# Shift and scale of six channel tiles by VectorE's product and sum, low parts of these rows on GpSimd, h by ScalarE

## The chip, the cores and the metric

The kernel runs on one core of one Trainium2 chip. The metric is the device time of one execution in microseconds (us). A core has five engines that run their own instruction rows and wait for each other by semaphores: TensorE (PE; its weight loads are shown as PEld), VectorE (DVE), ScalarE (ACT), GpSimd (POOL) and SyncE (SP), which here only issues transfers.

## What is computed

One layer of a trunk with two parallel head groups, a bidirectional state-space scan (SSD) and a gated MLP, over 256 latent tokens and 256 context tokens of 2048 channels. What matters here is its beginning: the modulation of the normalised rows and the first columns of the input projection.

```
shift, scale, gate       = split(silu(c)     @ w_ada + b_ada, 3)      # c: (2048,), w_ada: (2048, 3 * 2048)
shift_c, scale_c, gate_c = split(silu(c_ctx) @ w_ada + b_ada, 3)
hc = rmsnorm(ctx, g_pre) * (1 + scale_c) + shift_c
zc = hc @ w_in[:, :XBC_W + DT_W]
hx = rmsnorm(x, g_pre) * (1 + scale) + shift
zx = hx @ w_in
... scan, gating, output projection ...
return x + gate * rmsnorm(mixed, g_post)
```

All inputs are float32.

## The kernel before

The 2048 channels are 16 tiles of 128 (kt = 0 to 15), with channels on partitions; the 512 tokens (context, then latent) are columns. Every matrix product of the projections is made of three products of rounded halves: hi is the value rounded by ScalarE (`copy` to fp32r), lo the rest (`tensor_tensor`, subtract), and `mm3` (L136) adds hi x hi, hi x lo and lo x hi.

The front of the program, up to `st.close()`, goes like this. x is loaded in four pieces, squared (on VectorE and ScalarE by turns, L264 and L266) and summed over channels by products with ones (L268); `rb` (L282) is the root-mean-square factor of each token, the same in all partitions, kept in a segment of `y`, a tile that is not in use yet. Between the groups of products stand products of ones as warm-up (`warm`).

Then the streamed projections run over kt. `row_steps` (L325) writes out the order for TensorE, VectorE, ScalarE and GpSimd by hand, one list of steps per channel tile:

- `("a", ci)` is `ada_mm` (L204): one chunk of w_ada, 1 MiB, against silu(c) and silu(c_ctx) on TensorE. A unit of `UNITS` is one or two channel tiles; it sums shift and scale of its tiles over all 2048 rows of w_ada in one PSUM bank, four groups of partitions side by side. Two chunks belong to a tile.
- `("f", u)` is `ada_fin` (L218): VectorE transposes the bank in blocks of 32 (L222) into `adat`, ScalarE makes from it ha = g_pre * (1 + scale) (L224) and hb = shift (L226), each 128 x 2 for the two token halves.
- `("h", kt)` is `make_h` (L304): for each half VectorE makes x * ha * rb (L307), ScalarE adds hb and rounds (hhi, L310), VectorE makes the rest hlo (L312).
- `("s", kt)` is `split_st` (L294): ScalarE rounds the row of w_in for dt and seven column tiles (`wst`, 128 x 960, L299), VectorE makes its low parts (L300, L301).
- `("m", i)` are the products, psdt (L362, L363) first and then seven psx tiles.

A list ends each step with the rest of its "m". In the last one, `dt_tok` copies psdt out and multiplies it by `fold` (pstok, L320), a sum of two halves of the identity that is made at L165.

SyncE's row of loads is in program order: `ada_load` and `wst_load` stand ahead of each kt, three chunks and two w rows ahead; six buffers hold w_ada chunks, three hold w rows. Then the program goes on with the other columns of w_in as a stream of 1 MiB tiles w (hi_w, lo_w), the scan, the gating and the output projection. There, for `gate`, VectorE already makes the third part of c @ w_ada by itself (`gate_tile`, L884): w_ada's columns lie on partitions, the row of silu(c) is broadcast to all partitions, and one `scalar_tensor_tensor` with `accum_out` multiplies and sums along 2048 values.

Of the kernel before, what the change touches and what calls it, by code (L numbers as in the profile page):

```python
# [29 lines left out]
WSSD = (0, 1, 2, 3, 4, 12, 5, 6, 13, 7, 8, 14, 9, 10, 15, 11)  # L30
C_BADA, C_GPRE, C_GSSD, C_GMLP, C_BS, C_CW, C_CB, NPC = 0, 48, 64, 80, 96, 112, 272, 304
# [10 lines left out]
def tile_hybrid_ssd_mlp(  # L42
# [88 lines left out]
    cpool.tile([P, 64], F32, name="cpad")  # L131
# [32 lines left out]
    A = yseg(7)[:, 320:384]  # L164
    nc.vector.tensor_reduce(fold, ident.rearrange("p (g m) -> p m g", g=2), axis=mybir.AxisListType.X, op=ALU.add)  # L165
# [12 lines left out]
    sc2 = stp.tile([P, KT, 2], F32, name="sc2")  # L178
    nc.sync.dma_start(sc2, ccols)
# [5 lines left out]
    ada_raw = {}  # L185


    UNITS = [(0,), (1,)] + [(m, m + 1) for m in range(2, KT, 2)]

    def ada_place(ci):  # L190

        if ci < 4:
            return ci // 2, 64, 8 * (ci % 2), 8
        return ci // 4 + 1, 128, 4 * (ci % 4), 4

    def ada_load(*cs):
        for ci in cs:
            ada_raw[ci] = load_raw(wada[ci], f"ada_{ci}")
# [6 lines left out]
    def ada_mm(ci):  # L205
        u, n, k0, nk = ada_place(ci)
        if k0 == 0:
            ada_ps[u] = spt([P, 512], f"psada{u}")
        ps = ada_ps[u]
        raw = ada_raw.pop(ci)  # L210
        for kk in range(nk):
            k = k0 + kk
            for g in range(4):
                o = (kk * 4 + g) * n
                nc.tensor.matmul(ps[32 * g : 32 * g + 32, 0:n], lhsT=sc[:, k, :], rhs=raw[:, o : o + n],  # L215
                                 start=k == 0, stop=k == KT - 1)

    def ada_fin(u):  # L218
# [4 lines left out]
        for q, kt in enumerate(UNITS[u]):  # L223
            nc.scalar.activation(ha[:, kt, :], tr[:, 64 * q : 64 * q + 2], AF.Identity, bias=bsc1[:, kt : kt + 1],  # L224
                                 scale=pc[:, C_GPRE + kt : C_GPRE + kt + 1])
            nc.scalar.activation(hb[:, kt, :], tr[:, 64 * q + 32 : 64 * q + 34], AF.Identity,  # L226
                                 bias=pc[:, C_BADA + kt : C_BADA + kt + 1])
# [5 lines left out]
    wraw = {}  # L233

    def wst_load(kt):
        w = st3.tile([P, WST], F32, tag="wst", name=f"wst{kt}")
        nc.sync.dma_start(w, wst[kt])
        wraw[kt] = w

    for t in range(4):  # L240
        nc.sync.dma_start(xT[:, 4 * t : 4 * t + 4, :].rearrange("p k t -> p (k t)"), xch[t])
    ada_load(0)
    wst_load(0)
    ada_load(1, 2, 3)
    wst_load(1)
    ada_load(4, 5)

# [9 lines left out]

    warm(2)

    pss = spt([P, TOK], "pss")  # L260
    for k in range(KT):
        sq = yseg((1, 2, 3, 6, 0)[k % 5])
# [6 lines left out]
        if g == 3:  # L269
            warm(1)  # L270


    rb, ss4 = yseg(4), yseg(5)
# [9 lines left out]
    ada_mm(0)  # L283
    ada_mm(1)
# [10 lines left out]
    def split_st(kt):  # L295
# [4 lines left out]
        nc.vector.tensor_tensor(hi[:, 0:64], raw[:, 0:64], hi[:, 64:P].bitcast(F32), op=ALU.subtract)  # L300
        nc.vector.tensor_tensor(lo, raw[:, 64:], hi[:, P:].bitcast(F32), op=ALU.subtract)  # L301
        return hi, lo

    def make_h(kt):  # L304
        sl = (slice(256, 512), slice(0, 256))
        for v, s in enumerate(sl):
            nc.vector.scalar_tensor_tensor(xT[:, kt, s], xT[:, kt, s], ha[:, kt, v : v + 1], rb[:, s],  # L307
                                           op0=ALU.mult, op1=ALU.mult)
        for v, s in enumerate(sl):
            nc.scalar.activation(hhi[kt][:, s], xT[:, kt, s], AF.Identity, bias=hb[:, kt, v : v + 1])  # L310
        for v, s in enumerate(sl):
            nc.vector.scalar_tensor_tensor(hlo[kt][:, s], xT[:, kt, s], hb[:, kt, v : v + 1],  # L312
                                           hhi[kt][:, s].bitcast(F32), op0=ALU.add, op1=ALU.subtract)


    def dt_tok():
        nc.scalar.copy(zdt, psdt)
# [7 lines left out]
    def row_steps(kt):  # L325
# [3 lines left out]
        nxt = [("h", kt + 1), ("s", kt + 1)]  # L329
        if kt == 0:  # L330
            return m[:1] + [("a", 2)] + m[1:2] + [("a", 3)] + m[2:3] + [("f", 1)] + nxt + m[3:] + [("a", 4), ("a", 5)]
        if kt < 3:
            f = [("f", 2)] if kt == 1 else []
            return m[:3] + [("a", 2 * kt + 4)] + m[3:5] + [("a", 2 * kt + 5)] + f + nxt + m[5:]
# [6 lines left out]
        a = [("a", 2 * kt + 4), ("a", 2 * kt + 5)] if kt + 2 < KT else []  # L341
        f = [("f", (kt + 1) // 2 + 1)] if kt % 2 else []
        if kt < 5:
            return m[:2] + a + f + nxt + m[2:]
        return nxt[1:] + a + f + nxt[:1] + m

    def step(kt, what, i):
        if what == "a":
            ada_mm(i)
# [4 lines left out]
        elif what == "s":  # L354
            sp0[i] = split_st(i)
# [13 lines left out]
    sp0[0] = split_st(0)  # L369
    ada_fin(0)  # L370
    make_h(0)
    for kt in range(KT):
        if kt + 3 < KT:
            ada_load(2 * kt + 6, 2 * kt + 7)
        if kt + 2 < KT:
            wst_load(kt + 2)
# [4 lines left out]
        for what, i in row_steps(kt):  # L381
            step(kt, what, i)
# [772 lines left out]
def _layout(i):  # L1155
# [13 lines left out]
    for kt in range(2):  # L1169
        wada[2 * kt : 2 * kt + 2] = ss[:, :, :, kt].reshape(2, 8, P, 256).transpose(0, 2, 1, 3).reshape(2, P, D)  # L1170
# [50 lines left out]
```

## Time and profile before

| | us |
|---|---|
| median of 3 runs (1000.07 to 1000.66) | 1000.56 |
| the profiled execution | 999.99 |
| its span, first to last instruction | 998.3 |
| TensorE busy, share of the span | 977.1 (98%) |
| VectorE busy | 629.9 (63%) |
| ScalarE busy | 493.0 (49%) |
| GpSimd busy | 113.7 (11%) |
| streamed projections' end, first product of the w stream | 134.00 |

The profile is of one execution. Its views: a page of the whole span; the timeline (start in us, length in us, engine, line, operation, out<-in, shape, count, and in brackets the idle time before it and what ended it); stretches of the span with the busy time of each engine; and one line's instructions with their shortest, median and longest duration in ns. A VectorE instruction with `accum_out` shows as two, the second of which reads the accumulator (DVE_READ_ACCUMULATOR). Names are the program's tiles without their numbers.

### The profile page before, as it was taken

To read this page: it belongs to the slowest core of one execution; us is meant where nothing else is said; L and a number is where in the kernel's file an instruction comes from. 1 tells how busy PE (TensorE), PEld (TensorE's weight loads), DVE (VectorE), ACT (ScalarE), POOL (GpSimd) and SP (SyncE) were. 2 spreads that over 40 slices of the span, in tenths; PEclk is the share of its full clock that TensorE was granted. 3 is DMA by queue.
4 is the path that set the end of the run, shared out by engine and by line. 5 is a ranking of instruction groups with operands and counts; after the bars stand their busy time and mean duration, and the time that the engine had idled before them with its cause. 6 is when DMAs were issued, how large, how long until landed. Compare 5 with 4: busy or idle time off the path is not lost.

```text
span 998.3 us, 14183 instructions
## 1 busy us (share of the span) xinstructions
PE 977.1 (98%) x5636; PEld 791.3 (79%) x5636; DVE 629.9 (63%) x944; ACT 493.0 (49%) x759; POOL 113.7 (11%) x162
## 2 busy tenths in 40 slices
PE   7999999999999999999999999999999999999996
PEld 3788888778687878787888888877888888888885
DVE  4344478877977665666667766666565564445636
ACT  4233347666656545544445343455565564346522
POOL 0000003423443222224000000000000000000000
PEclk9999999999999999999999999999999999999998
DMA  9999744333224323235878778674555545556722
GB/s 380 419 417 419 293 175 143 111 127 127 85 85 165 103 112 133 79 127 195 311 283 297 275 258 319 252 274 172 185 173 191 188 169 209 175 207 231 274 85 84
DMA packets 31554, 207.28 MB, mean 208 GB/s; under 512 B 4080, under 2 KB 4208, under 8 KB 7808
## 3 DMA queue, kind: packets, MB, share of 16 engines
q1 hardware_dynamic: 28656, 192.52, 51.5%
q0 software_dynamic: 2112, 12.65, 3.6%
q10 hardware_dynamic: 720, 1.20, 0.3%
q8 instruction: 44, 0.72, 0.3%
q14 instruction: 22, 0.18, 0.1%
HBM read 204.20 MB, written 2.16 MB: 207 GB/s over the span
## 4 chain that ended last, share of the span: by engine, by line
PE 69%; issue 11%; DMA 9%; DVE 8%; POOL 1%; ACT 1%; SPq 0%; DVEq 0%; POOLq 0%; ACTq 0%
PE psx L138 9%; PE psx L140 9%; PE psx L139 9%; PE pa L1026 5%; PE pa L1028 5%; PE pa L1027 5%; DMA gate<-in_wada_dram 5%; PE pm L1073 3%; PE pm L1075 3%; PE pm L1074 3%; PE psada L215 3%; DVE xbc L495 2%; PE pq L1075 2%; PE pq L1073 2%; PE pq L1074 2%
## 5 line engine op out<-in xcount | busy, mean ns | idle before, releaser
L82 DVE TENSOR_TENSOR lo_w<-w,hi_w 128x1024 fp32r<-128x1024 f32 x173 | 210.5, 1224 | 144.3 <-ACT hi_w L81 144.3
L81 ACT CAST hi_w<-w 128x1024 fp32r<-128x1024 f32 x173 | 182.1, 1053 | 202.5 <-PE pa L1028 130.5
L1026 PE MATMUL pa<-hi_w,hhi 128*128 128x512 f32 x512 | 202.5, 395 | 0.0
L1028 PE MATMUL pa<-hi_w,hlo 128*128 128x512 f32 x512 | 199.5, 390 | 0.0
L1027 PE MATMUL pa<-lo_w,hhi 128*128 128x512 f32 x512 | 199.4, 389 | 0.0
L138 PE MATMUL psx<-hhi,hi_w 128*128 128x512 f32 (+1 forms) x400 | 153.5, 384 | 1.3 <-DVE xbc L495 1.3
L140 PE MATMUL psx<-hhi,lo_w 128*128 128x512 f32 (+1 forms) x400 | 146.0, 365 | 0.0
L139 PE MATMUL psx<-hlo,hi_w 128*128 128x512 f32 (+1 forms) x400 | 145.7, 364 | 0.0
L1026 PEld LDWEIGHTS pa<-hi_w,hhi 128*128 128x128 f32 x512 | 96.2, 188 | 20.7 <-issue 1.6
L1028 PEld LDWEIGHTS pa<-hi_w,hlo 128*128 128x128 f32 x512 | 96.1, 188 | 20.2
L1027 PEld LDWEIGHTS pa<-lo_w,hhi 128*128 128x128 f32 x512 | 96.2, 188 | 19.4 <-issue 0.2
L495 DVE SCALAR_TENSOR_TENSOR xbc<-psx,pc,xbc 128x248 f32<-128x248 f32 (+1 forms) x204 | 83.6, 473 | 36.6 <-ACT xbc L479 35.6
L420 DVE TENSOR_TENSOR lo_w<-w,hi_w 128x1024 fp32r<-128x1024 f32 x61 | 78.1, 1287 | 25.0 <-ACT hi_w L414 25.0
L138 PEld LDWEIGHTS psx<-hhi,hi_w 128*128 128x128 f32 x400 | 75.5, 189 | 15.0 <-issue 3.1
L140 PEld LDWEIGHTS psx<-hhi,lo_w 128*128 128x128 f32 x400 | 75.4, 189 | 12.6
L139 PEld LDWEIGHTS psx<-hlo,hi_w 128*128 128x128 f32 x400 | 75.6, 189 | 12.1 <-issue 1.7
L414 ACT CAST hi_w<-w 128x1024 fp32r<-128x1024 f32 x61 | 63.4, 1044 | 26.4 <-PE pa L1028 13.3
L884 DVE SCALAR_TENSOR_TENSOR junk<-gate,cb 128x2048 bf16<-128x2048 f32 x16 | 36.6, 2290 | 24.6 <-DMA gate<-in_wada_dram 24.6
L1073 PE MATMUL pm<-hi_w,hhi 128*128 128x512 f32 x128 | 50.0, 390 | 0.0
L1074 PE MATMUL pm<-lo_w,hhi 128*128 128x512 f32 x128 | 49.9, 390 | 0.0
L1075 PE MATMUL pm<-hi_w,hlo 128*128 128x512 f32 x128 | 49.7, 389 | 0.0
L138 PE MATMUL psx<-hhi,hi_st 128*128 128x512 f32 (+1 forms) x112 | 41.3, 369 | 0.0
(219 smaller groups left out, 1333.7 us busy)
## 6 DMA issues: line engine op xcount, KB each, us to landing
w<-in_wlat_dram SPq DMA_DIRECT2D x64, 1024.0 KB, 4.8
ada<-in_wada_dram SPq DMA_DIRECT2D x32, 1024.0 KB, 14.6
w<-in_wout_dram SPq DMA_DIRECT2D x32, 1024.0 KB, 4.8
w<-in_wxbc_dram SPq DMA_DIRECT2D x25, 1024.0 KB, 4.8
gate<-in_wada_dram SPq DMA_DIRECT2D x16, 1024.0 KB, 5.7
R<-acs POOLq DMA_DIRECT2D x8, 1024.0 KB, 4.9
wst<-in_wst_dram SPq DMA_DIRECT2D x16, 480.0 KB, 14.8
xT<-in_xch_dram SPq DMA_DIRECT2D x4, 1024.0 KB, 8.0
```

Source lines behind the costliest of these rows:

```text
L81: nc.scalar.copy(hi, raw)
L82: nc.vector.tensor_tensor(lo, raw, hi.bitcast(F32), op=ALU.subtract)
L138: nc.tensor.matmul(ps, lhsT=whi, rhs=hhi[k][:, s], start=start, stop=False)
L139: nc.tensor.matmul(ps, lhsT=whi, rhs=hlo[k][:, s], start=False, stop=False)
L140: nc.tensor.matmul(ps, lhsT=wlo, rhs=hhi[k][:, s], start=False, stop=stop)
L495: nc.vector.scalar_tensor_tensor(ao, zi, cw[:, k : k + 1], ao, op0=ALU.mult, op1=ALU.add)
L1026: nc.tensor.matmul(pa[tk], lhsT=hhi[k][:, t], rhs=whi[:, w], start=k == 0, stop=False)
L1027: nc.tensor.matmul(pa[tk], lhsT=hhi[k][:, t], rhs=wlo[:, w], start=False, stop=False)
L1028: nc.tensor.matmul(pa[tk], lhsT=hlo[k][:, t], rhs=whi[:, w], start=False, stop=k == KT - 1)
L1073: nc.tensor.matmul(p, lhsT=yh[:, t], rhs=whi[:, w], start=j == 0, stop=False)
L1074: nc.tensor.matmul(p, lhsT=yh[:, t], rhs=wlo[:, w], start=False, stop=False)
L1075: nc.tensor.matmul(p, lhsT=yl[:, t], rhs=whi[:, w], start=False, stop=hf == 0 and j == 15)
```

## The change

For six channel tiles (5, 7, 9, 11, 13, 14: `VTILES`) shift and scale are no longer made on TensorE. Their columns of w_ada are laid out as those of the gate are, channels on partitions: chunk v.0 holds the scale columns and v.1 the shift columns of a tile. VectorE multiplies each chunk with the rows of silu(c) and silu(c_ctx) and sums along the 2048 rows (`ada_v`, two per chunk, four per tile) into `vsum`, and `ada_vfin` makes ha and hb from it. The ten others stay with TensorE, as units of one tile but for the pair (2, 3).

The broadcast rows of silu(c) and silu(c_ctx) are made at the start: products of a column with the identity in PSUM (`c_rows`, in place of the warm-up between the groups), copied by ScalarE into `y` (`c_keep`). Therefore `rb` and the scratch of the squares' sum move to a tile `junk4`, which is also the scratch output of the products and sums; `fold` is made in `dt_tok`, since its place in `y` is taken; A has a tile of its own.

The rows of x are multiplied by rb at once, eight on VectorE and eight on GpSimd (`norm`). `make_h` then has ScalarE make h = x * ha + hb: for kt under 4 rounded from x, with VectorE making the same once more in full; from 4 on in place, with a rounded copy after. VectorE makes one subtraction for hlo over all 512 tokens. The low parts of `split_st` go from VectorE to GpSimd, and a row is split two steps ahead instead of one. Loads are issued by a list, `LOADS`, as soon as a buffer is given back.

```
+UNITS = ((0,), (1,), (2, 3), (4,), (6,), (8,), (10,), (12,), (15,))
+VTILES = (5, 7, 9, 11, 13, 14)
+
+LOADS = "u0.0 w0 u0.1 u1.0 u1.1 w1 w2 u2.0 u2.1 u2.2 u2.3 w3 w4 v5.0 v5.1 u3.0 u3.1 w5 w6 v7.0 v7.1 u4.0 u4.1 w7 w8 " \
+        "v9.0 v9.1 u5.0 u5.1 w9 w10 v11.0 v11.1 u6.0 u6.1 w11 w12 v13.0 v13.1 u7.0 u7.1 w13 w14 v14.0 v14.1 w15 u8.0 u8.1"
...
+    junk4 = stp.tile([P, D // 2], F32, name="junk4")
+    junk, rb, ss4 = junk4.bitcast(BF16), junk4[:, 0:512], junk4[:, 512:1024]
...
+    def ada_v(kt, c, v):
+        raw = ada_raw[f"v{kt}.{c}"]
+        nc.vector.scalar_tensor_tensor(junk, raw, 1.0, y[:, v, :], op0=ALU.mult, op1=ALU.mult,
+                                       accum_out=vsum[:, kt, c, v : v + 1])
+        if v == 1:
+            give("a")
...
+    def c_rows(*bs):
+        for b in bs:
+            p = acp.tile([P, 512], F32, tag="acc", name=f"psr{b}")
+            for q in range(4):
+                k = 4 * (b % 4) + q
+                nc.tensor.matmul(p[:, q * P : (q + 1) * P], lhsT=sc[:, k, b // 4 : b // 4 + 1].to_broadcast([P, P]),
+                                 rhs=ident, start=True, stop=True)
+            cbp[b] = p
...
-        nc.vector.tensor_tensor(hi[:, 0:64], raw[:, 0:64], hi[:, 64:P].bitcast(F32), op=ALU.subtract)
-        nc.vector.tensor_tensor(lo, raw[:, 64:], hi[:, P:].bitcast(F32), op=ALU.subtract)
-        return hi, lo
+        nc.gpsimd.tensor_tensor(hi[:, 0:64], raw[:, 0:64], hi[:, 64:P].bitcast(F32), op=ALU.subtract)
+        nc.gpsimd.tensor_tensor(lo, raw[:, 64:], hi[:, P:].bitcast(F32), op=ALU.subtract)
+        sp0[kt] = hi, lo
+        give("w")
+
+    def norm(eng, *ks):
+        for k in ks:
+            eng.tensor_tensor(xT[:, k, :], xT[:, k, :], rb, op=ALU.mult)
...
     def make_h(kt):
...
+            full = x
+            for v, s in enumerate(sl):
+                nc.scalar.activation(x[:, s], x[:, s], AF.Identity, bias=hb[:, kt, v : v + 1], scale=ha[:, kt, v : v + 1])
+            nc.scalar.copy(hhi[kt], x)
+        nc.vector.tensor_tensor(hlo[kt], full, hhi[kt].bitcast(F32), op=ALU.subtract)
...
     def dt_tok():
+        nc.vector.tensor_reduce(fold, ident.rearrange("p (g m) -> p m g", g=2), axis=mybir.AxisListType.X, op=ALU.add)
         nc.scalar.copy(zdt, psdt)
...
+        nv = 5 + (kt - 2) // 2 * 2 if kt < 12 else 14
+        if kt % 2 == 0:
+            return [("v", nv, 0, 0), ("s", kt + 2), ("v", nv, 0, 1)] + m
+        if kt == KT - 3:
+            return [("v", nv, 1, 0), ("v", nv, 1, 1), ("V", nv), ("h", nv), ("s", kt + 2)] + m
+        u = 3 + (kt - 3) // 2
+        return ([("v", nv, 1, 0)] + m[:1] + [("a", u, 0)] + m[1:3] + [("a", u, 1), ("f", u), ("h", kt + 1)]
+                + [("s", kt + 2), ("v", nv, 1, 1), ("V", nv), ("h", nv)] + m[3:])
...
+    split_st(0)
+    c_keep(6, 7)
+    norm(nc.vector, 0)
+    norm(nc.gpsimd, 1, 2, 3)
     ada_fin(0)
     make_h(0)
+    split_st(1)
+    norm(nc.gpsimd, 4, 5, 6, 7, 8)
+    norm(nc.vector, 9, 10, 11, 12, 13, 14, 15)
```

How this moves instructions, at three places. VectorE's row for the two steps in which h of tiles 8 and 9 is made, before (adat5 is the transposed bank of that pair of tiles):

```order
L300 TENSOR_TENSOR hi_st8_931<-wst8_856,hi_st8_931 128x64
L301 TENSOR_TENSOR lo_st8_932<-wst8_856,hi_st8_931 128x896
L222 STREAM_TRANSPOSE adat5_968<-psada5_863 128x128
L307 SCALAR_TENSOR_TENSOR xT_156<-xT_156,ha_111,y_68 128x256 x2
L312 SCALAR_TENSOR_TENSOR hlo8_141<-xT_156,hb_110,hhi8_125 128x256 x2
L300 TENSOR_TENSOR hi_st9_1009<-wst9_929,hi_st9_1009 128x64
L301 TENSOR_TENSOR lo_st9_1010<-wst9_929,hi_st9_1009 128x896
L307 SCALAR_TENSOR_TENSOR xT_156<-xT_156,ha_111,y_68 128x256 x2
L312 SCALAR_TENSOR_TENSOR hlo9_142<-xT_156,hb_110,hhi9_126 128x256 x2
```

The same place now (ada_v9_0 and ada_v9_1 are the two chunks of tile 9, junk4 the scratch output):

```order
L244 SCALAR_TENSOR_TENSOR junk4_161,vsum_166<-ada_v9_0_755,y_68 128x2048 x2
L244 SCALAR_TENSOR_TENSOR junk4_161,vsum_166<-ada_v9_1_758,y_68 128x2048
L261 STREAM_TRANSPOSE adat5_1045<-psada5_970 128x64
L371 TENSOR_TENSOR hlo8_141<-xT_155,hhi8_125 128x512
L244 SCALAR_TENSOR_TENSOR junk4_161,vsum_166<-ada_v9_1_758,y_68 128x2048
L371 TENSOR_TENSOR hlo9_142<-xT_155,hhi9_126 128x512
```

The low parts of the w rows and the products with ha and rb are gone from VectorE, four products and sums of 2048 values have come, and each hlo is one instruction that stands between them.

ScalarE's row at that place, now:

```order
L250 ACTIVATE ha_111<-adat5_1045,bsc1_112,pc_87 128x2
L252 ACTIVATE hb_110<-adat5_1045,pc_87 128x2
L369 ACTIVATE xT_155<-xT_155,hb_110,ha_111 128x256 x2
L370 CAST hhi8_125<-xT_155 128x512
L344 CAST hi_st9_1053<-wst9_854 128x960
L250 ACTIVATE ha_111<-vsum_166,bsc1_112,pc_87 128x2
L252 ACTIVATE hb_110<-vsum_166,pc_87 128x2
L369 ACTIVATE xT_155<-xT_155,hb_110,ha_111 128x256 x2
L370 CAST hhi9_126<-xT_155 128x512
L344 CAST hi_st10_1087<-wst10_907 128x960
```

h itself and its rounded copy have come to ScalarE, ahead of each rounding of a w row, and the second ha and hb read vsum.

GpSimd, which had nothing between its constants and the scan, has this row at its start now:

```order
L345 TENSOR_TENSOR hi_st0_362<-wst0_176,hi_st0_362 128x64
L346 TENSOR_TENSOR lo_st0_363<-wst0_176,hi_st0_362 128x896
L352 TENSOR_TENSOR xT_155<-xT_155,junk4_161 128x512 x3
L345 TENSOR_TENSOR hi_st1_384<-wst1_184,hi_st1_384 128x64
L346 TENSOR_TENSOR lo_st1_385<-wst1_184,hi_st1_384 128x896
L352 TENSOR_TENSOR xT_155<-xT_155,junk4_161 128x512 x5
L345 TENSOR_TENSOR hi_st2_489<-wst2_186,hi_st2_489 128x64
L346 TENSOR_TENSOR lo_st2_490<-wst2_186,hi_st2_489 128x896
```

Eight rows of x by rb (in junk4) stand among the first low parts; after them one pair of low parts follows for each w row.

152 lines of the change are left out of this document (84 added, 68 removed).

## The prediction

> **What bounds the kernel now.** First the stretches of the span, since the change lies in the first 134 us alone:
>
> ```profile
> 0.00:40.00 40.00, 34.52 (x476) 19.41 (x477) 15.89 (x35) 13.37 (x27) 2.37 (x15) 1.00 0.96 395
> 40.00:119.00 79.00, 77.42 (x1026) 63.92 (x1024) 37.86 (x79) 28.55 (x59) 0.00 (x0) 1.00 0.93 383
> 119.00:134.00 15.00, 15.00 (x86) 12.71 (x79) 8.91 (x18) 8.51 (x16) 0.00 (x0) 1.00 0.71 281
> ```
>
> The columns are stretch, length, busy time of PE, PEld, DVE, ACT and POOL, granted clock, DMA share and GB/s. From 40 to 119 us TensorE and the transfers are both nearly full (77.42 of 79.00 us; 0.93), VectorE is half idle, GpSimd does nothing. Then the timeline of TensorE gives the pace:
>
> ```profile
> 83.55 1.95 PE L215 MATMUL psada<-ada,sc 128*32 128x128 f32 x64
> 90.28 1.96 PE L215 MATMUL psada<-ada,sc 128*32 128x128 f32 x64
> 119.10 0.50 PE L362 MATMUL psdt<-hhi,hi_st 128*128 128x512 f32 x1
> 128.47 0.40 PE L362 MATMUL psdt<-hhi,hi_st 128*128 128x512 f32 x1
> 134.00 0.40 PE L138 MATMUL psx<-hhi,hi_w 128*128 128x512 f32 x1
> ```
>
> A channel tile takes 6.73 us (90.28 less 83.55), 13.46 a pair; without shift-and-scale products 4.68 (half of 128.47 less 119.10); the last, with its small products, 5.53. So a chunk of w_ada costs TensorE 0.98 us, and the streamed projections begin at 134.00 without a wait. From there TensorE is the limit to the end, so what the front gains or loses reaches the end whole.
>
> The transfers' own pace shows where TensorE waits for a chunk:
>
> ```profile
> 26.27 1.10 PE L215 MATMUL psada<-ada,sc 128*32 128x64 f32 x64
> 32.41 0.81 PEld L215 LDWEIGHTS psada<-ada,sc 128*32 128x32 f32 x32 [0.61 <-DMA ada<-in_wada_dram]
> ada<-in_wada_dram SPq DMA_DIRECT2D x32, 1024.0 KB, 14.6
> wst<-in_wst_dram SPq DMA_DIRECT2D x16, 480.0 KB, 14.8
> ```
>
> Two chunks and one w_st tile (2.47 MiB) land in 6.14 us: 2.49 us per MiB. A pair of tiles (4.94 MiB) needs 12.3 us, which the change leaves as it is.
>
> **What leaves TensorE.** Twelve chunks at 0.98 us, 11.8 us. By itself that lets a pair run at the transfers' 12.3 us. The eight c_rows groups of products stand where the warm-up products stood, while x is still landing: nothing, within a microsecond either way.
>
> **What VectorE gets.** The gate's product and sum has the very form of the new one, and these rows price the rest:
>
> ```profile
> L884 DVE SCALAR_TENSOR_TENSOR junk<-gate,cb x16: 2284/2292/2294, 478.5 to 650.6; 128x2048 bf16<-128x2048 f32 x16
> L884 DVE DVE_READ_ACCUMULATOR junk<-gate,cb x16: 80/83/84, 480.7 to 652.8; 128x1 f32 x16
> L222 DVE STREAM_TRANSPOSE adat<-psada x9: 249/318/318, 21.0 to 119.2; 128x128 f32<-128x128 f32 x7, 128x64 f32<-128x64 f32 x2
> L264 DVE TENSOR_TENSOR y<-xT x8: 684/690/693, 6.3 to 14.3; 128x512 f32<-128x512 f32 x8
> 119.59 0.39 ACT L224 ACTIVATE ha<-adat,bsc,pc 128x2 f32<-128x2 f32 x1 [4.55 <-DVE adat L222]
> 119.88 0.28 ACT L226 ACTIVATE hb<-adat,pc 128x2 f32<-128x2 f32 x1
> 120.59 0.91 ACT L310 ACTIVATE hhi<-xT,hb 128x256 fp32r<-128x256 f32 x2
> L317 ACT COPY y<-psdt x1: 588/588/588, 129.1 to 129.1; 128x512 f32<-128x512 f32 x1
> L299 ACT CAST hi_st<-wst x16: 975/988/998, 17.5 to 121.4; 128x960 fp32r<-128x960 f32 x16
> ```
>
> One product and sum costs 2.29 + 0.08 for its accumulator, 2.40 with the hand-off, since each waits for the one before (one scratch tile). Four per pair are 9.6 us. VectorE loses its w_st low parts and the two h operations per half, and keeps one 0.69 us subtraction per tile. Its busy time, some 11.2 of 12.3 us, would fit. Its order decides: it now stands in line behind ScalarE twice a pair. In an odd step the row runs: transpose (0.25); ScalarE's ha, hb (0.57), h in two halves (0.91) and rounded copy (0.59), 2.2 with hand-offs; subtraction (0.69); the pair's fourth product and sum (2.40), behind which hb, h and copy of the next tile come once more (1.9); subtraction (0.69); then three products and sums (7.2) ahead of the next transpose. VectorE holds the later ones back while it waits. The sum is 0.25 + 2.2 + 0.69 + 2.4 + 1.9 + 0.69 + 7.2 = 15.3 us, above the 13.46 of before. TensorE's second chunk is done some 10 to 13 us into this circle, so it doesn't lengthen it.
>
> **What GpSimd gets.** Each step's low parts, 128x64 and 128x896, and eight rows of x by rb. No row has these shapes; the nearest:
>
> ```profile
> L764 POOL TENSOR_TENSOR y<-y,yo x32: 724/739/3995, 196.4 to 465.6; 128x256 f32<-128x256 f32 x32
> L725 POOL TENSOR_TENSOR M<-cbb,dtt x16: 1032/1040/1042, 184.9 to 456.8; 128x512 f32<-128x512 f32 x16
> L626 POOL TENSOR_TENSOR xw<-xk,ed x32: 602/612/1645, 164.1 to 434.0; 128x256 f32<-128x256 f32 x32
> ```
>
> From L626 to L725 256 columns add 0.43 us, so 896 would take 1.68; 3.5 times L764 is 2.59. I take 2.15 (L764, like the new one, reads two whole tiles; its 0.74 less a start of 0.18, scaled), 1.3 for 512 and 0.3 for 64: 4.9 us a pair, which alone would hide in VectorE's waits. But the maxima, twice and five times the medians, say that GpSimd was held up, and the timeline shows by whom:
>
> ```profile
> 168.60 2.61 POOL L742 TENSOR_TENSOR y<-xk,dsk 128x256 f32<-128x256 f32 x2
> 168.31 0.86 DVE L656 TENSOR_TENSOR E<-R 128x512 f32<-128x512 f32 x1
> 169.10 1.63 DVE L420 TENSOR_TENSOR lo_w<-w,hi_w 128x1024 fp32r<-128x1024 f32 x1
> 170.66 1.10 DVE L656 TENSOR_TENSOR E<-R 128x512 f32<-128x512 f32 x1
> L420 DVE TENSOR_TENSOR lo_w<-w,hi_w x61: 1207/1219/1758, 132.3 to 468.7; 128x1024 fp32r<-128x1024 f32 x61
> L656 DVE TENSOR_TENSOR E<-R x16: 679/701/1224, 168.3 to 420.2; 128x512 f32<-128x512 f32 x16
> 298.99 4.00 POOL L764 TENSOR_TENSOR y<-y,yo 128x256 f32<-128x256 f32 x1 [1.26 <-DVE yo L756]
> ```
>
> Between 168.3 and 171.8 the two engines take turns: lo_w takes 1.63 instead of 1.22, E 1.10 instead of 0.70, two GpSimd rows of 0.61 last 2.61. The last E ends at 171.76, 0.55 after GpSimd's end at 171.21, so some 0.15 us of the blocked one's 0.70 was already spent. At 298.99 one GpSimd row waited 4.00 us, while VectorE's operations followed one another without a gap.
>
> The Trainium skill (SBUF — State Buffer, "SBUF: two separate sides") states that GpSimd and a VectorE operation with two SBUF inputs share one port pair as an exclusive lock, held for the whole instruction by whichever starts first. The rows agree but for that 0.15 us; with the whole instruction counted, this page makes the sum below some 3 us longer.
>
> Every product and sum and every subtraction of the new row reads two tiles from SBUF. Between two products and sums lies the accumulator's 0.08 us and a wait, a gap into which a waiting GpSimd row can step. After the copy of an odd step ScalarE rounds the next w_st, 0.99 us later GpSimd wants hi and lo while VectorE runs products and sums: hi (0.15 net) and lo (2.0 net) go ahead of one each. The other low part falls into the second wait for ScalarE and overhangs it by 0.35. A pair takes 15.3 + 2.5 = 17.8 us.
>
> **The sum.** The circle turns from f3 (transpose for tile 4) to f7 (tile 12), four times. f3: chunk u2.3 lands at 26.27 + 4.94 x 2.49 = 38.6, TensorE has it at 39.6. Transpose, four small ScalarE rows, h in halves and subtraction bring h of tile 2 to 42.6, h of tile 3 to 44.5. Three products and sums make it 51.7; u3.1 (9.87 MiB behind 26.27, plus 0.98) allows 51.9. So 52 without collisions. GpSimd puts its last row of x and low part 2 ahead of tile 2's subtraction, low part 3 ahead of tile 3's, hi and low part 4 between the products, some 2 us each: 58. f7 is 58 + 4 x 17.8 = 129.2. From there: h of tile 13 after 8.5; tile 14's four products and sums with one hi and lo 11.8; ScalarE and subtraction 2.6; TensorE to u8's second chunk 4.3 (at 27.2); transpose to h of tile 15 3.2; the last tile 5.3. That is 35.7. Then the end of the front:
>
> ```profile
> L165 DVE TENSOR_REDUCE y<-ident x1: 281/281/281, 7.5 to 7.5; 128x64 f32<-128x128 f32 x1
> 129.83 1.37 DVE L357 COPY y<-psx 128x512 f32<-128x512 f32 x2 [4.27 <-PE psx L140]
> 130.31 1.00 PE L320 MATMUL pstok<-y 128*128 128x64 f32 x8
> w<-in_wxbc_dram SPq DMA_DIRECT2D x25, 1024.0 KB, 4.8
> ```
>
> The fold was done at 7.5 us; now it stands behind the two copies, and the small products need it: they would start at 129.83 + 1.37 + 0.28 = 131.5 instead of 130.31, 1.2 us later. The front ends at 129.2 + 35.7 + 1.2 = 166.1 instead of 134.0: 32.1 us later. Order and transfers of what follows are unchanged; its first w tile, whose load waits for the chunk at 27.2, lands 4.8 later, 5 us before it is needed.
>
> The profiled execution took 999.99 us with a span of 998.3, 0.57 below the median of 1000.56; so 999.99 + 32.1 = 1032.
>
> **What the clock may add.** The granted clock is 1.00 in every stretch above, in which TensorE idles 5.5 of the first 40 us and 1.6 of the next 79; in the forecast it idles some 5 us at a time, once a pair. The Trainium skill (TensorE: Matmul & The Clock Gate, "Part 1") states that after an idle window of about 3.4 us the clock is half until as much busy time has passed. No run here shows it; its cost, an estimate from that page, is 1.7 us per gap, hidden in the circle's waits except once at the end.
>
> **The rivals.** *No collisions cost* (GpSimd's rows fit into VectorE's waits): 52 + 4 x 15.3 + 34.4 = 147.6, 13.6 later, 1014 us. For it: 4.1 us of waits stand against 4.9 of GpSimd rows. Against it: the turns at 168 us. Were GpSimd kept out between products and sums, as at 298.99, the pair would be near 16 and the result 1024, inside my forecast's own 1024 to 1040 (low parts at 1.68 or 2.59 move it by 5).
>
> *Faster: the transfers set the pace.* If the circle came under 12.3 us, TensorE would wait for chunks alone: u7's second chunk at 26.27 + 29.6 x 2.49 = 100.0, then its 0.98, the step's rest 2.5, two tiles 9.4, tile 14 up to its last chunk 4.5, h of tile 15 3.2, last tile 6.7: 127.3, 6.7 earlier, 993 us. It needs the product and sum at 1.6 us instead of 2.40, or the ScalarE waits filled; the row's order speaks against both.
>
> *Much slower:* GpSimd's rows cost more than 2.59, or collisions delay each subtraction too, or the clock drops: 19.5 a pair and a later start, over 1043.
>
> *The change doesn't do what it says:* the moved work is in the order, so only a chance balance gives no difference; 0.2%, 2 us, is what a measurement here can tell.
>
> **Chances.** Forecast 0.56 (1024 to 1040), no collisions 0.22 (about 1014), faster 0.10, much slower 0.10, balance 0.02. The range 1010 to 1043 leaves out the last three. Faster 0.10, same 0.02, slower 0.88.
>
> **What would show it.** In the new profile: products and sums near 2.3 us, or lengthened by GpSimd's low parts; the transposes of psada 15 to 18 us apart from about 58 us on; VectorE idle until ScalarE's rounded copy twice a pair; TensorE idle some 5 us a pair until hlo; GB/s lower than 380 from 60 us on; the first hi_w product near 166 us. Transposes 12.3 us apart with TensorE waiting for ada chunks would prove me wrong, as would a low part on GpSimd that runs beside a product and sum without either growing.

## The result, and the profile after

| | before | after |
|---|---|---|
| median, us | 1000.57 (1000.07 to 1000.66) | 1036.33 (1033.9 to 1037.86) |
| ratio, 95% interval | | 1.0356 (1.0334 to 1.0379) |
| the profiled execution | 999.99 | 1035.36 |
| its span | 998.3 | 1033.6 |
| first product of the w stream | 134.00 | 165.06 |
| from there to the end | 864.30 | 868.54 |

The front is 31.06 us longer, what follows it 4.24. The stretches of the front in after (columns as in the prediction):

```profile
40.00:119.00 79.00, 67.41 (x812) 52.38 (x811) 54.24 (x53) 30.33 (x59) 50.17 (x21) 0.91 0.81 319
119.00:165.06 46.06, 33.70 (x383) 26.18 (x381) 28.02 (x30) 16.73 (x30) 18.32 (x8) 0.89 0.48 191
```

From 40 to 119 us TensorE is busy for 67.41 us instead of 77.42, and 319 GB/s come in instead of 383: neither limit of before is reached any more. The engine that turns is VectorE. One circle of its row in after, transpose to transpose (the lines left out are the readings of the accumulator, 0.08 us each):

```profile
75.66 0.24 DVE L261 STREAM_TRANSPOSE adat<-psada 128x64 f32<-128x64 f32 x1
78.31 0.69 DVE L371 TENSOR_TENSOR hlo<-xT,hhi 128x512 fp32r<-128x512 f32 x1 [2.41 <-ACT hhi L370]
78.92 2.29 DVE L244 SCALAR_TENSOR_TENSOR junk<-ada_v,y 128x2048 bf16<-128x2048 f32 x1
...
83.36 0.69 DVE L371 TENSOR_TENSOR hlo<-xT,hhi 128x512 fp32r<-128x512 f32 x1 [2.15 <-ACT hhi L370]
83.97 2.29 DVE L244 SCALAR_TENSOR_TENSOR junk<-ada_v,y 128x2048 bf16<-128x2048 f32 x1
...
86.30 2.29 DVE L244 SCALAR_TENSOR_TENSOR junk<-ada_v,y 128x2048 bf16<-128x2048 f32 x1
...
88.63 4.09 DVE L244 SCALAR_TENSOR_TENSOR junk<-ada_v,y 128x2048 bf16<-128x2048 f32 x1
...
92.65 0.24 DVE L261 STREAM_TRANSPOSE adat<-psada 128x64 f32<-128x64 f32 x1
```

GpSimd's row in the same circle:

```profile
79.25 2.14 POOL L345 TENSOR_TENSOR hi_st<-wst,hi_st 128x64 fp32r<-128x64 f32 x1 [5.67 <-ACT hi_st L344]
81.36 2.13 POOL L346 TENSOR_TENSOR lo_st<-wst,hi_st 128x896 fp32r<-128x896 f32 x1
84.30 2.14 POOL L345 TENSOR_TENSOR hi_st<-wst,hi_st 128x64 fp32r<-128x64 f32 x1 [0.82 <-ACT hi_st L344]
86.40 4.17 POOL L346 TENSOR_TENSOR lo_st<-wst,hi_st 128x896 fp32r<-128x896 f32 x1
```

A pair of tiles takes 16.99 us, here and on the mean of the four circles. VectorE stands still for ScalarE twice (2.41, 2.15), and one product and sum of four takes 4.09 us instead of 2.29. Reading both rows together: hi at 79.25 shows 2.14 us because it waits until the product of 78.92 ends at 81.2, its own work is 0.3 (0.32 at 19.98, where nothing stands in its way); lo at 81.36 runs in VectorE's second wait; hi at 84.30 waits likewise and is done at 86.4, and the product that starts at 86.30 keeps its 2.29; lo at 86.40 waits for that product, runs from 88.6 to 90.6, and the product of 88.63 shows that wait as its own time.

The start, VectorE's row in before and in after (the transposes of psada only, and what stands ahead of them):

```profile
16.15 0.72 DVE L274 STREAM_TRANSPOSE y<-pss 128x512 f32<-128x512 f32 x1 [1.14 <-PE pss L268]
...
20.97 0.25 DVE L222 STREAM_TRANSPOSE adat<-psada 128x64 f32<-128x64 f32 x1 [0.67 <-PE psada L215]
...
27.43 0.25 DVE L222 STREAM_TRANSPOSE adat<-psada 128x64 f32<-128x64 f32 x1 [3.75 <-PE psada L215]
...
38.88 0.32 DVE L222 STREAM_TRANSPOSE adat<-psada 128x128 f32<-128x128 f32 x1 [7.10 <-PE psada L215]
```

```profile
17.54 0.72 DVE L318 STREAM_TRANSPOSE junk<-pss 128x512 f32<-128x512 f32 x1 [1.77 <-PE pss L310]
...
20.61 2.30 DVE L352 TENSOR_TENSOR xT<-xT,junk 128x512 f32<-128x512 f32 x1
24.57 0.25 DVE L261 STREAM_TRANSPOSE adat<-psada 128x64 f32<-128x64 f32 x1 [1.67 <-PE psada L234]
...
27.66 9.56 DVE L352 TENSOR_TENSOR xT<-xT,junk 128x512 f32<-128x512 f32 x7
37.14 0.24 DVE L261 STREAM_TRANSPOSE adat<-psada 128x64 f32<-128x64 f32 x1
...
45.14 0.32 DVE L261 STREAM_TRANSPOSE adat<-psada 128x128 f32<-128x128 f32 x1 [4.54 <-PE psada L234]
```

The sums of squares end 1.4 us later, the transposes for tiles 0, 1 and 2 come 3.6, 9.7 and 6.3 us later. For tile 1 VectorE waits for nobody: seven rows of x by rb stand ahead of it, 1.37 us each beside GpSimd's.

### The profile page after: what moved, and what is told of

It reads as the page before. It is cut to its first block, busy times and chain, and to the rows that moved or that the text cites. A ratio compares the mean times of both kernels' runs of the same rounds, so it can differ in the third digit from the quotient of the medians.

```text
span 1033.6 us, 14363 instructions
## 1 busy us (share of the span) xinstructions
PE 984.8 (95%) x5692; PEld 794.5 (77%) x5692; DVE 674.0 (65%) x929; ACT 508.0 (49%) x779; POOL 200.1 (19%) x202
## 4 chain that ended last, share of the span: by engine, by line
PE 59%; DVE 13%; issue 13%; DMA 6%; ACT 3%; POOL 1%; DVEq 0%; ACTq 0%; POOLq 0%
PE psx L144 7%; PE psx L146 7%; PE psx L145 7%; PE pa L1095 5%; PE pa L1097 5%; PE pa L1096 5%; DMA gate<-in_wada_dram 5%; DVE junk L244 5%; PE pm L1144 3%; PE pm L1143 3%; PE pm L1142 3%; DVE xbc L564 2%; PE pq L1144 2%; PE pq L1143 2%; DVE lo_w L88 2%
## 5 line engine op out<-in xcount | busy, mean ns | idle before, releaser
L564 DVE SCALAR_TENSOR_TENSOR xbc<-psx,pc,xbc 128x248 f32<-128x248 f32 (+1 forms) x204 | 83.6, 473 | 36.9 <-ACT xbc L548 36.0
L483 ACT CAST hi_w<-w 128x1024 fp32r<-128x1024 f32 x61 | 63.4, 1045 | 26.3 <-PE pa L1097 13.3
L244 DVE SCALAR_TENSOR_TENSOR junk<-ada_v,y 128x2048 bf16<-128x2048 f32 x24 | 65.6, 2734 | 0.5
```

Source lines behind the costliest of these rows:

```text
L244: nc.vector.scalar_tensor_tensor(junk, raw, 1.0, y[:, v, :], op0=ALU.mult, op1=ALU.mult, accum_out=vsum[:, kt, c, v : v + 1])
L564: nc.vector.scalar_tensor_tensor(ao, zi, cw[:, k : k + 1], ao, op0=ALU.mult, op1=ALU.add)
```

## The experiments

Each is compared with the kernel before on its own chip. "Start of the w stream" is the first hi_w product of the profile.

**e1_no_lows: after without GpSimd's low parts.**

```
-        nc.gpsimd.tensor_tensor(hi[:, 0:64], ...); nc.gpsimd.tensor_tensor(lo, ...)
+        lo = hi[:, P:]
...
-            nc.tensor.matmul(psdt, lhsT=whi[:, 0:P], ...)
+            nc.tensor.matmul(psdt, lhsT=whi[:, 64:P + 64], ...)
```

The rounded row stands in for the low parts, so TensorE has the same products, but the result is no longer the layer's.

> The changed kernel with GpSimd's low parts of the w_st tiles left out: the third product of each pair takes the rounded tile in their place, so TensorE has the same products and the output is another one. Theory of the line (VectorE's row sets the pace, and a GpSimd row costs it time only where it steps in ahead of a waiting VectorE operation): the product and sum that took 4.07 us falls to 2.29, a pair of tiles from 16.97 to 15.2 us; five such places behind 56 us and one before it give 6 x 1.77 = 10.6 us, and the rows of x by rb, which still share the time with GpSimd, give up to 1 us more as a low part stood among them. Streamed projections start near 154 us, time near 1025 us (1023 to 1028). Rival (the long product and sum waits for its own data or scratch tile, not for GpSimd): it stays at 4.07 us, time 1036 us.

Measured: 1023.72 us, ratio 1.0248 (1.0225 to 1.0271); w stream from 156.73. One circle's end points and the product that had been long:

```profile
71.24 2.29 DVE L244 SCALAR_TENSOR_TENSOR junk<-ada_v,y 128x2048 bf16<-128x2048 f32 x1
...
73.46 0.25 DVE L261 STREAM_TRANSPOSE adat<-psada 128x64 f32<-128x64 f32 x1
...
88.78 0.24 DVE L261 STREAM_TRANSPOSE adat<-psada 128x64 f32<-128x64 f32 x1
```

All 24 products take 2.28 or 2.29 us and the pair 15.2 to 15.3. The length was GpSimd's doing, 1.7 us a pair (16.99 less 15.28 on the mean of four circles); the row alone is still slower than the 13.46 of before.

**e2_rows_vector: all rows of x by rb on VectorE.** `norm(nc.gpsimd, ...)` becomes `norm(nc.vector, ...)` twice.

> The changed kernel with all sixteen rows of x by rb on VectorE, none on GpSimd. Theory of the shared port (a row of GpSimd takes from VectorE what it lasts): VectorE's eight rows took 2.30 and 9.56 us beside GpSimd's eight; sixteen alone are 16 x 0.62 to 0.69 = 9.9 to 11.0 us, so the transpose for tile 1 comes 0 to 2 us earlier than at 37.14 and the time is 1034 to 1037 us. Rival (GpSimd's rows run beside VectorE's for nothing, and VectorE's rows were slow there for another reason): eight rows more cost 5.5 to 11 us, the time is 1042 to 1047 us.

Measured: 1032.71 us, ratio 1.0333 (1.0308 to 1.0359), under the expected range; the rival's 1042 to 1047 us are out.

```profile
23.24 4.10 DVE L352 TENSOR_TENSOR xT<-xT,junk 128x512 f32<-128x512 f32 x4
27.27 0.24 DVE L261 STREAM_TRANSPOSE adat<-psada 128x64 f32<-128x64 f32 x1
...
29.88 9.34 DVE L352 TENSOR_TENSOR xT<-xT,junk 128x512 f32<-128x512 f32 x12
39.15 0.24 DVE L261 STREAM_TRANSPOSE adat<-psada 128x64 f32<-128x64 f32 x1
```

Twelve rows in 9.34 us where seven took 9.56: from transpose to transpose 11.88 us instead of 12.57, and from the transpose of the sums of squares (at 20.17) to that for tile 1 18.98 us instead of 19.60. GpSimd's eight rows brought tile 1 no earlier. In time e2 and after can't be told apart, since the intervals of their ratios overlap.

**e3_fill: one product and sum into each wait for ScalarE.**

```
-  f(u) h(kt+1) s  v(1,1) V h(nv)  |  v(0,0) s v(0,1)
+  f(u) H(kt+1) s  v(1,1) l(kt+1) V H(nv)  |  v(0,0) l(nv) s v(0,1)
```

H is ScalarE's part of `make_h`, l VectorE's subtraction; the bar is the next step.

> The changed kernel with VectorE's order altered alone: between the transpose (or the last sum) and the subtraction that waits for ScalarE stands one product and sum. Theory of the line: the two waits of 2.4 and 2.1 us in a pair are filled; the row is 0.25 + 2 x 0.69 + 4 x 2.40 = 11.2 us, but GpSimd then finds no idle VectorE, and both low parts of a pair cost 1.8 us each: 14.8 us instead of 16.97. Over four pairs and a half 9 to 10 us: time near 1027 us (1024 to 1030). Rival 1 (GpSimd finds its time between the products and sums): 12.3 to 13 us a pair, the transfers' pace, time near 1017 us. Rival 2 (the order isn't what costs; ScalarE's chain or the port is full): 16.5 us a pair or more, time 1034 to 1037 us.

Measured: 1025.7 us, ratio 1.0271 (1.0246 to 1.0296).

```profile
84.76 2.56 DVE L376 TENSOR_TENSOR hlo<-xT,hhi 128x512 fp32r<-128x512 f32 x1 [0.25 <-ACT hhi L370]
...
89.69 4.07 DVE L244 SCALAR_TENSOR_TENSOR junk<-ada_v,y 128x2048 bf16<-128x2048 f32 x1
```

The waits are down to 0.25 us, the pair takes 14.74 to 14.76 from 78.93 us on (the first circle, 62.50 to 78.93, takes 16.43), and both low parts now stand ahead of a VectorE instruction: a subtraction of 2.56 instead of 0.69, a product of 4.07.

**e4_lows_vector: low parts back on VectorE, order as in after.** `nc.gpsimd` becomes `nc.vector` in `split_st`.

> The changed kernel with the w_st low parts back on VectorE, in the same place of its row, and the rest as changed. VectorE took 0.15 + 1.05 us for one in the kernel before. Theory of the line: the row is the 15.2 us without collisions + 2 x 1.2 + a short wait for the rounding = 17.8 to 18.0 us a pair, 0.9 us more than the measured 16.97; time near 1039 us (1036 to 1042). Rival (GpSimd's rows cost VectorE more than the one long product shows): the pair gets shorter than 16.97 us and the time is under 1034 us. Rival (the low parts were free on GpSimd): 2.5 us more a pair, time over 1045 us.

Measured: 1038.74 us, ratio 1.0397 (1.038 to 1.0413); the transposes are 17.64 to 17.77 us apart, just under the expected 17.8 to 18.0. In this order GpSimd was worth 0.7 us a pair; in after's rows above one of its two low parts runs in a wait.

**e5_fill_no_lows and e6_fill_lows_vector: the filled order, with the low parts left out (as in e1) and with them on VectorE** (there the low part stands behind the product that follows the rounding).

> VectorE's filled order of the run before, and GpSimd's low parts of w_st left out (the rounded tile stands in for them in the third products, so the output is another one). Theory: the filled row took 14.74 us a pair, with both low parts ahead of a VectorE operation at 1.8 us each; without them it is 11.15, and the transfers' 12.3 us set the pace. Transposes 12.3 us apart from about 57 us on, two collisions less in the tail: streamed projections start near 139 us, time near 1006 us (1002 to 1010). Rival (something else than VectorE's row, such as ScalarE's chain or TensorE's clock, holds the pair at 14 us): time 1015 us or more.

Measured: 1007.17 us, ratio 1.0073 (1.0059 to 1.0086), w stream from 140.76.

> VectorE's filled order, with the low parts of w_st on VectorE. Theory: where VectorE has no idle time left, a low part on GpSimd takes 1.8 us from it, and its own takes 1.2: the row is 11.15 + 2 x 1.2 = 13.55 us a pair, 1.2 less than the 14.74 with GpSimd. Streamed projections start near 152 us, time near 1018 us (1014 to 1022), 8 below the filled order with GpSimd. Rival (GpSimd's rows are still the cheaper place): time above 1025.7 us.

Measured: 1016.03 us, ratio 1.0157 (1.0138 to 1.0176), w stream from 150.93. The four circles of the first in one stretch, and a circle of the second:

```profile
55.63:107.90 52.27, 48.84 (x697) 38.52 (x697) 42.15 (x44) 25.12 (x48) 0.00 (x0) 1.00 0.99 408
```

```profile
90.08 0.24 DVE L261 STREAM_TRANSPOSE adat<-psada 128x64 f32<-128x64 f32 x1
...
103.22 0.24 DVE L261 STREAM_TRANSPOSE adat<-psada 128x64 f32<-128x64 f32 x1
```

Without low parts the transfers are full (0.99, 408 GB/s), and two of the four circles take their pace, 12.32 and 12.33 us (transposes at 68.91, 81.23, 93.56); the two others take 13.3 and 14.3. With them on VectorE a pair takes 13.1 us from the second circle on (the first takes 16.0), 1.6 less than with GpSimd. So the worth of GpSimd turns with the order: ahead by 0.7 us where VectorE has waits, behind by 1.6 where it has none.

**e7_three: three tiles instead of six.** `VTILES = (5, 9, 13)`, filled order, low parts and rows by rb on VectorE (these rows spread over the steps), one chunk at a time among the projections. The last two groups of c stand behind the first tile's chunks, tiles 0 to 3 have their h made as in before, and `fold` is made two tiles earlier.

> Three tiles (5, 9, 13) by VectorE's products and sums instead of six, the filled order, low parts and all rows of x by rb on VectorE (the rows spread over the steps, each three ahead), the last two groups of products of c behind the first chunk, the fold made two tiles earlier. Theory: in four tiles TensorE has 4 x 4.68 + 6 x 0.98 = 24.6 us, the transfers 24.6, VectorE 2 x 0.25 + 4 x (0.69 + 0.69 + 1.2) + 9.6 = 20.4 and no wait that isn't filled: 12.3 us a pair against 13.46 before. Six pairs give 7 us, the small waits take 1 to 2 back: streamed projections near 128.5 us, time 0.9945 of before (0.992 to 0.998). Rival (two limits at the same height don't both run full: a chunk that comes late isn't made up): no gain, 0.998 to 1.004. Rival (VectorE's line still comes late for TensorE): slower than before.

Measured: 1005.05 us, ratio 1.0054 (1.0041 to 1.0066): a miss. TensorE's row for one tile:

```profile
58.18 0.50 PE L452 MATMUL psdt<-hhi,hi_st 128*128 128x512 f32 x1 [1.06 <-ACT hhi L372]
...
58.90 0.50 PE L453 MATMUL psdt<-hlo,hi_st 128*128 128x512 f32 x1 [0.23 <-DVE hlo L378]
...
60.03 1.08 PE L234 MATMUL psada<-ada_u,sc 128*32 128x128 f32 x32
...
62.98 1.08 PE L234 MATMUL psada<-ada_u,sc 128*32 128x128 f32 x32
...
65.86 0.40 PE L452 MATMUL psdt<-hhi,hi_st 128*128 128x512 f32 x1
```

This tile took 7.68 us and the next 7.4 where before took 6.73: h comes late, and each chunk breaks the row of projections once more. Four tiles take 27.14 us (55.49 to 82.63), 13.57 a pair.

**e9_three_paired: chunks in twos ahead of a tile's projections, h right behind.**

> Three tiles by products and sums as in the run before, with the chunks of w_ada in twos ahead of a tile's projections, as in the kernel before, and h made right behind them. Theory: a chunk that stands alone among the projections cost TensorE 1.2 us instead of 0.98, and the late h 1.5 us in four tiles; without both, four tiles take 4 x 4.65 + 6 x 1.0 = 24.7 us on TensorE and 24.6 in the transfers, against 26.9 before. From 55 us on three such groups give 6 us: streamed projections near 129 us, time 0.995 of before (0.992 to 0.998). Rival (the transfers, full from 20 to 110 us in both kernels, set the end, and TensorE waits for chunks where it used to be late): 0.998 to 1.004. Rival (VectorE's row with two products and sums between the transpose and the next tile's subtraction comes late for TensorE once in four tiles): like the run before, 1.004 to 1.007.

Measured: 998.32 us, ratio 0.9988 (0.998 to 0.9997), w stream from 132.45: outside the expected 0.992 to 0.998, within the first rival's range.

```profile
56.59 0.24 DVE L261 STREAM_TRANSPOSE adat<-psada 128x64 f32<-128x64 f32 x1
...
80.84 0.24 DVE L261 STREAM_TRANSPOSE adat<-psada 128x64 f32<-128x64 f32 x1
...
105.09 0.24 DVE L261 STREAM_TRANSPOSE adat<-psada 128x64 f32<-128x64 f32 x1
```

24.25 us for four tiles, 12.1 a pair: the pace is there, and the circle gains what was expected. The start gives most of it back: the transpose for tile 2 stands at 43.59 instead of 38.88. Part of that can be this execution's: the granted clock is 0.50 from 8.03 to 11.44 us here, while in e7, where it was 1.00 from 5.0 us up to 25.5, the transpose for tile 2 stands at 42.48.

**e11_three_start and e12_three_squares: c's eight groups of products moved about in the start.** In e11 two groups each among the squares at two places, behind the first chunks and behind the first dt product; in e12 two of them go from the squares to behind these, and the squares have six buffers.

> The last version (three tiles, chunks in twos) with the products of c spread over the start: two groups each at the two first places among the squares, two behind the first tile's chunks in place of the warm-up products, two behind the first dt product. Theory: c's products ahead of the last squares and behind the first chunks made the transposes for tiles 0, 1 and 2 late by 2.4, 5.2 and 4.7 us against the kernel before, and the end only 1.55 us early; with them out of the way the start is 2 to 3 us earlier and the streamed projections start near 129.5 us; 0.996 of before (0.994 to 0.998). Rival (the transfers set the start, which are full from 20 us on): the transpose for tile 2 stays at 42 to 44 us and the time at 0.9985 to 1.0.

Measured: 997.33 us, ratio 0.9975 (0.9965 to 0.9985), w stream from 132.43, transpose for tile 2 at 44.10.

> The last version with only two of c's eight groups among the squares, the next two behind the last squares, and six row buffers for the squares instead of four. Theory: TensorE's products of c stood ahead of the products of the next squares, and these squares waited for their buffers, so the sums of squares ended at 19.5 us instead of the 16.15 of before; now they end at 16.2 to 17.2, the transposes for tiles 0 to 2 come 2 us earlier than in the last version, and the streamed projections start near 130.5 us; time 0.995 to 0.997 of before. Rival (the chunks' transfers set the transposes for tiles 1 and 2, whatever the squares do): the transpose for tile 2 stays at 43.5 to 44.1 us and the streamed projections start at 132.4.

Measured: 996.89 us, ratio 0.9974 (0.9964 to 0.9984), w stream from 132.69, transpose for tile 2 at 44.37. TensorE's products of c in e12:

```profile
9.40 3.79 PE L292 MATMUL psr<-ident,sc 128*128 128x128 f32 x16
...
18.25 2.05 PE L292 MATMUL psr<-ident,sc 128*128 128x128 f32 x16
...
22.28 2.05 PE L292 MATMUL psr<-ident,sc 128*128 128x128 f32 x16
...
26.87 3.58 PE L292 MATMUL psr<-ident,sc 128*128 128x128 f32 x16
```

Both expected an earlier start, and the profiles don't show it: in both the transpose for tile 2 stayed behind that of e9, so e11's time lies in its expected range without the reason given for it, and e12's just above its own. Of the 11.5 us of c's products in e12 the last three entries, 7.7, stand between the sums of squares and the second tile, where TensorE is busy for 18.3 of 20 us (18.46 to 38.46). Some of that is the clock: it is 0.50 from 26.88 to 30.29 us in this profile, and the group at 26.87 takes 3.58 us instead of 2.05. Whether TensorE's own work, its clock or the transfers (share 1.02 in these 20 us) set that start was not told apart. Both versions beat the kernel before by 0.25%; that the second is better than the first is within the intervals.

**e10_c_later: after, the last two groups of c behind the first tile's chunks.**

> The changed kernel with the last two groups of products of c behind the first tile's chunks on TensorE, and their copies behind the first h on ScalarE. Theory: these groups (2.0 us at 18.6) made the first transpose late by 1.7 us (VectorE waited 1.67 for it at 24.57) and with it VectorE's whole row; the first transpose comes 1.7 us earlier after the transpose of the sums of squares (5.3 behind it instead of 7.0), and the streamed projections as much earlier. Rival (VectorE's rows of x by rb set the pace there): the second transpose stays 19.6 us behind that of the sums of squares, no gain.

Measured: 1035.81 us, ratio 1.0353 (1.0337 to 1.0369). The first transpose comes 5.28 us behind that of the sums of squares (19.30, 24.58) instead of 7.03, the second 20.05 behind it (39.35) instead of 19.60. The rival holds: an earlier first transpose brings the second no earlier. VectorE's rows of x by rb, which stand ahead of it, set it.

**e8_before_lows_pool: the kernel before, with the low parts on GpSimd and nothing else.**

> The kernel before with one part of the change alone: the low parts of w_st on GpSimd. Theory: VectorE has 6 to 7 us idle in a pair there and TensorE sets the pace, so the rows that GpSimd holds up, 1.8 us at most each, are hidden: no difference, within 0.2% of before. Rival (holding the port delays h and the low parts come 1 us later, and TensorE waits for them once a tile): 1 us a tile, 12 us or 1.2% slower.

Measured: 1003.63 us, ratio 1.0036 (1.0024 to 1.0048), w stream from 137.10: neither answer. From 68 us on the pace is that of before (81.94, 95.40, 108.87, 122.33: 13.46 a pair), although VectorE's second h operation takes 881 ns on average (before: 484). The 3.1 us are lost ahead of that, at tiles 2 and 4. One product of TensorE and its weight loads there, and the same ones in before:

```profile
43.31 0.63 PE L138 MATMUL psx<-hhi,hi_st 128*128 128x512 f32 x1
44.40 0.28 PEld L140 LDWEIGHTS psx<-hhi,lo_st 128*128 128x128 f32 x1 [0.76 <-POOL lo_st L301]
...
60.45 0.19 PEld L140 LDWEIGHTS psx<-hhi,lo_st 128*128 128x128 f32 x1 [1.31 <-POOL lo_st L301]
...
60.88 1.69 PEld L215 LDWEIGHTS psada<-ada,sc 128*32 128x32 f32 x64 [0.24 <-issue]
```

```profile
42.91 0.39 PE L138 MATMUL psx<-hhi,hi_st 128*128 128x512 f32 x1
43.34 0.19 PEld L140 LDWEIGHTS psx<-hhi,lo_st 128*128 128x128 f32 x1 [0.24 <-DVE lo_st L301]
...
57.33 0.19 PEld L140 LDWEIGHTS psx<-hhi,lo_st 128*128 128x128 f32 x1 [0.24 <-DVE lo_st L301]
...
57.77 1.69 PEld L215 LDWEIGHTS psada<-ada,sc 128*32 128x32 f32 x64 [0.25 <-issue]
```

There a low part is made just before it is needed, and GpSimd's 2.1 us stand in TensorE's way instead of VectorE's 1.08. At tile 2 the clock has a part in it: it is 0.50 from 42.43 to 45.84 us, behind a stretch as long in which TensorE was busy for 1.48 us, and a product takes 0.63 us. The first product with a low part comes 1.06 us later than in before (44.40, 43.34), the chunk behind it 1.71 (46.17, 44.46); the 0.65 between are lost without a wait for GpSimd. In before the stretch from 39.41 to 42.82 was busy for 1.83 us and kept its clock. Whether other executions lose these 0.65 us too isn't shown.

## Why the prediction was right, and where it was not

- **VectorE's order decides, not its busy time.** Right: e1, with the low parts gone, measures the row alone at 15.2 to 15.3 us (forecast 15.3), and e3, which alters the order alone, takes 2.2 us a pair off. The row's terms were each a little off: with its hand-off a product and sum took 2.33 us (83.97 to 86.30) and not 2.40, and in e1 the waits for ScalarE are 2.48 and 2.20 us instead of 2.2 and 1.9.
- **The price of a product and sum.** Right: 2.29 + 0.08, as in the gate. A chunk's price on TensorE was read too low: 6.73 less 4.68 is 2.05 for two chunks, so 1.02 each; 0.98 is the length of their products alone. The sum uses it for single chunks only, so it moves little.
- **The collisions.** Right in kind, too high in size: 1.7 us a pair instead of 2.5. "Hi (0.15 net)" cost nothing measurable, and the low part that was to overhang the second wait by 0.35 fitted in. The pair took 16.99 instead of 17.8. The rival without collisions is refuted by e1. The Trainium skill (SBUF — State Buffer, "SBUF: two separate sides") has the pair of ports held for the whole instruction, which here takes 2.10 us alone (20.26). The product grew by 1.76 to 1.80 us (4.05 to 4.09 less 2.29), so the measurement is 0.3 us below that.
- **The start.** f3 at 58.64 (forecast 58) was right by two errors. "TensorE has it at 39.6" failed: the transpose for tile 2 came at 45.14. The step that failed has two parts. The rows of c were put at "nothing, within a microsecond", and tile 0's transpose came 3.6 us late; and VectorE's seven rows of x by rb, 9.56 us ahead of tile 1's transpose, were not in the sum at all (e10: they set it; e2: without GpSimd's share it comes no later). They aren't all of it: in e7, whose sums of squares end where after's do (17.57), these rows are spread out and tile 1's transpose comes at 32.30 instead of 37.14, yet tile 2's still at 42.48, 3.6 us behind before's. What sets that rest stays open. Against the lateness, from f2 to f3 I had put some 18.4 us with three collisions of about 2, and it took 13.5 with one product of 4.07.
- **The tail.** 38.5 us from f7 to the w stream, forecast 36.9. Nearly all of the difference is one step: from h of tile 14 to the transpose for tile 15, 6.15 us instead of 4.3, at half clock (below). The clock's estimate of 1.7 us "except once at the end" was stated and left out of the sum; it belonged in it. That the rest hides in the circle's waits was right: the circle from 75.66 to 92.65, at full clock, takes 16.99 us, the next one, at half clock from 93.5 to 100.3, 16.97.
- **Behind the front.** "Order and transfers of what follows are unchanged" is true of the order, yet 4.24 us came there. At 688 us TensorE waits 2.9 us for VectorE's vt, which stands behind the last chunk of the gate, and the clock is 0.66 in the 5 us after; before, that wait was 0.7. It isn't the front's lateness: with the w stream from 168.50 (e2) there is no such wait, and 863.5 us follow. In the profiles without it 863.2 to 864.7 us follow, in the five with it 864.3 to 868.5. Why the gate's last chunk lands late in some executions stays open.
- **Faster, had the waits been filled.** That rival's condition fell short: e3 filled the waits and came to 14.74 us, because GpSimd then found no idle VectorE. With six tiles only the kernel without low parts (e5) came to the transfers' pace, and in two circles of four.

The errors nearly cancel: f3 0.6 late, four circles 3.3 early, the tail 1.6 late, behind the front 4.2 late; 3.1 in all, and the profiled 1035.36 stands against 1032 (the median of 1036.33 is 4.3 above it). That the sum came so near is in part luck. What isn't luck is that VectorE's row sets the circle, at 15.3 us without GpSimd, and that GpSimd's low parts lengthen it.

## What to carry to other kernels

Before work is given to an engine that is half idle, write out its row with what each instruction waits for: here the new work fitted VectorE's idle time, but two waits in its row made a circle of 15.2 us out of 11.1 us of work. An operation that goes from VectorE to GpSimd with two tiles from SBUF helped here only while it fell into VectorE's waits; where there were none, a low part on GpSimd cost VectorE 1.8 us instead of the 1.2 that its own took. And at the start, where little is made ahead, a slower engine on the way to the products costs time even when it is free later (e8).

## What the runs showed of the hardware

**The clock falls behind stretches that are about half busy or less, and it follows late.** In after's front the granted clock is 0.50 from 25.3, 62.8, 93.5, 114.0, 131.1 and 144.7 us on, for 3.41 or 6.83 us; these times lie whole multiples of 3.41 us apart:

```profile
110.60:114.00 3.40, 1.46 (x5) 1.04 (x6) 1.73 (x2) 2.79 (x5) 0.79 (x1) 1.00 1.00 417
114.00:117.40 3.40, 3.40 (x11) 2.76 (x11) 1.26 (x3) 2.13 (x5) 3.40 (x2) 0.50 0.17 63
...
144.70:151.60 6.90, 3.38 (x37) 2.19 (x41) 1.96 (x3) 2.90 (x5) 2.37 (x2) 0.51 0.00 0
```

TensorE idled 2.60 us up to 112.38, worked at full clock until 114.0, and only then fell to half, for 3.4 us of full work. The stretch before the fall was busy for 1.46 of 3.40 us. In the front of all the profiles, the first 9 us aside, every such stretch at full clock with TensorE busy for 1.54 us or less is followed by half clock, and none busy for more than 1.82 is; between them both occur. The way back needs more: behind 2.93 us (e10, from 82.62) and 3.05 us (e4, from 119.04) of work at half clock the clock stayed at half for another stretch. The Trainium skill (TensorE: Matmul & The Clock Gate, "Part 1") has a free-running window of 3.4 us, which agrees, and an idle window as the condition. This trace needs less: gaps of 1.43 and 0.17 us around 60 us sufficed (the stretch was busy for 1.82 us), while one of 1.13 at 77.3 did not (2.12 us).

**The first products are as fast as the clock of that execution.** In after, e5 and e7 the granted clock is 1.00 from 5 us on, the first products of c take 2.05 us, and the transpose of the sums of squares that wait behind them comes at 17.54 to 17.59. In e1, e6, e9 and e10 the clock is 0.50 for 3.41 us from 7.5 to 8.0 us on; there these products take 2.74 to 3.19 us and the transpose comes at 19.16 to 19.31. In e2, e3, e4, e11 and e12 they take 2.40 to 3.79 us, but those traces hold no record of the clock before 10.0 to 13.2 us. In both profiles without c's products the transpose comes at 16.02 and 16.15. How much of the times' scatter that makes isn't shown: the four runs of after lie 4.0 us apart and those of before beside them 0.6, but twelve runs of before on another chip lie 3.4 apart.

**TensorE stops without a wait, most likely for its own instructions.** Seven products before the end of tile 0's second chunk it stands still for 1.7 to 2.1 us in after and in e1 to e6, and the profile names no releaser ("issue"):

```profile
24.20 0.32 PE L234 MATMUL psada<-ada_u,sc 128*32 128x64 f32 x7 [1.77 <-issue]
```

It isn't that product: the stop stands behind the 223rd matmul of the trace, and in e7, e9 and e10, whose row is another, behind the 223rd again, among the products of c (2.4 to 2.7 us). In after, e2 and e3 a second stop of 1.5 to 2.3 us follows 128 matmuls later. On the DMA queue that the profile calls "instruction" (q8) a packet of 16,384 bytes is under way from 21.89 to 22.94 us in after, and in each of these thirteen stops TensorE goes on 1.2 to 1.6 us after such a packet has ended. The DMA engines are full then (share 0.99 from 21 to 25 us in after). No run changed that transfer, so the cause is read from the times and not tested.
